# Time mixing of an RWKV-7 layer: six slots per pair of heads in place of eight

## The chip, the cores and the metric

The kernel runs on one core of a Trainium2 chip. The metric is the time of one execution on the device, in microseconds (us). Before the change it is 2622.2 us, the median of three runs (2618.82 to 2623.88).

The engines of the core appear in the profile under short names: PE is the matrix engine (TensorE), PEld its loading of weights, DVE the vector engine, ACT the scalar engine, POOL GpSimd, SP the engine whose queue issues most of the DMAs. Each engine works through its own instructions in order and waits for the others by semaphores. Matmuls write to PSUM, which has eight banks; everything else lives in SBUF.

## The reference, cut to what matters

The model has two layers over 256 tokens of width 2048. The first layer mixes over time as below, the second by attention; each is followed by an MLP, and every sub-layer is shifted, scaled and gated by vectors made from `c` (adaLN). Only the time mixing matters here:

```python
def rwkv7_time_mix(h, mu, w_r, w_k, w_v, w_o, w0, w1, w2, a0, a1, a2,
                   g1, g2, k_k, k_a, r_k, ln_w, ln_b):
    ...
    r = xr @ w_r
    k = xk @ w_k
    v = xv @ w_v
    ...
    decay = jnp.exp(-jnp.exp(heads(w_log)))
    def step(S, inp):
        r_t, w_t, k_t, v_t, kk_t, a_t = inp
        sa = jnp.einsum('bhvk,bhk->bhv', S, -kk_t)
        S = (S * w_t[:, :, None, :] + sa[..., None] * (kk_t * a_t)[:, :, None, :]
             + v_t[..., None] * k_t[:, :, None, :])
        y = jnp.einsum('bhvk,bhk->bhv', S, r_t)
        return S, y
    ...
    _, y = lax.scan(step, S0, xs)
    ...
    y = ((y - mean) * lax.rsqrt(var + GN_EPS) * ln_w + ln_b)
    y = y + jnp.sum(r_h * k_h * r_k, axis=-1, keepdims=True) * v_h
    y = y.reshape(B, T, D).astype(h.dtype) * g
    return y @ w_o
```

There are 32 heads of 64 channels. The recurrence over tokens is written in chunks of 64: inside a chunk it is a triangular system, solved with an inverse; from chunk to chunk a 64 x 64 state is carried.

## The kernel before

**A pair.** The kernel takes two heads together, 128 channels on 128 partitions; there are 16 pairs (`NPAIR`). The class `Pair` (L78) writes the time mixing of one pair as a Python generator: each `yield` ends a step. There are three parts, `EARLY`, `INVERT`, `LATE` = 8, 12, 16 steps (L80). `early` (L152) makes decay, normalised keys and the tiles `kr`, `bh`, `kh`, `vp`, `bk`; the head sums of the keys and of the bonus (`pss`, `pbn`) are matmuls with a block of ones (`head_sums`, L138) on an operand split in two parts (`parts`, L142). `invert` (L228) forms the product `bh` x `kr`, takes its triangle, and builds the inverse by doubling in five levels of 32 x 32 products (`tiles`, L131); a level is two steps. At level 2 it also makes the masked product `mk` of `kh` and `kr`. `late` (L300) is the chain over the four chunks: the first product `g`, the inverse applied to it (`sa`), the output `y` and the next state `zs`; then the group norm of `y` (squares, head sums `var`, scale), the gate product `pg`, and the result in `v`.

**The slots.** The loop at L1019 sets the order of the work by hand. A pair starts `SLOTS` = 8 slots after the one before, so up to 4.5 pairs are under way; there are 8 x 16 + 36 = 164 slots. In a slot, each live pair issues one step: inverts first, then late steps, then early ones, the two `sums` steps of late at the end (L1027). Behind these steps follow dense matmuls to cover their latency: `proj_steps` (L962) gives the projections k and r of the next pair, 16 units of 6 matmuls a pair, two units a slot. `tc.issue_after` keeps this order in TensorE's queue. In the last 36 slots, the tail, the dense work is `out_steps` (L979), a part of the output projection, 56 units spread by `pace` (L1015). Behind a slot's work, in four slots of eight, `w_make` splits a half weight tile in two parts (`halves`, ACT L424 and DVE L427) and loads a further one; in six of eight, `ada` takes one step of the adaLN vectors of later layers (DVE L505), each with a 512 KB load into one of three buffers `rada`. `ADA_A` = 111 of these loads belong to this stage.

**PSUM.** The stage uses all eight banks: `pj` (projections, one), `ms` (two, by `psm`), `gr` (one tile of two banks, by `two`, L111), `iv` (one, by `corner`, L224), and `lt` (two, one bank per pair in `late`). In `late`, `lt` holds the chain's products, `y`, `var` and `pg`, so a pair holds its bank for 16 slots. In the tail the output projection takes over `pj`, `iv` and `gr`.

Of the kernel before, what the change touches and what calls it, by code (L numbers as in the profile page):

```python
# [25 lines left out]
C = 64  # L26
# [51 lines left out]
class Pair:  # L78

    EARLY, INVERT, LATE = 8, 12, 16  # L80
# [61 lines left out]
    def parts(self, src, t=None, func=AF.Copy, scale=1.0):  # L142
        nc = self.b.nc
        hl = self.b.pw.tile([P, 2, T], F32R, tag="sq", bufs=1, name="sq")
        nc.scalar.activation(hl[:, 0, :], src, func, scale=scale)
        if t is None:
            t = self.s()
            nc.scalar.activation(t, src, func, scale=scale)
        nc.vector.tensor_tensor(out=hl[:, 1, :], in0=t, in1=hl[:, 0, :], op=ALU.subtract)
        return hl  # L150

    def early(self):  # L152
# [25 lines left out]
        self.pc = pw.tile([P, 4, 1], F32, tag="pc", bufs=4, name="pc")  # L178
# [9 lines left out]
        self.bh, self.kh = s("bh", 2), s("kh", 2)  # L188
# [21 lines left out]
        nc.scalar.copy(self.even_odd(self.vp), self.by_chunk(pt, 2, C))  # L210
        yield
# [7 lines left out]
        pbn = b.psm()[:, :T]  # L219
        self.head_sums(pbn, rkp)  # L220
        nc.vector.tensor_tensor(out=v, in0=pbn, in1=v, op=ALU.mult)
        yield

    def corner(self, l):  # L224
        t = self.b.psm() if l == 5 or self.j >= NPAIR - 1 else self.b.pp.tile([P, 512], F32, tag="iv", bufs=1, name="iv")
        return t.rearrange("p (c t) -> p c t", t=H)[:, 0:4, :]

    def invert(self):  # L228
# [14 lines left out]
        ar = self.ar = s("ar", 3)  # L243
# [27 lines left out]
        for l in range(1, 6):  # L271
            xs = half("xs", 2)
            pi = self.corner(l)
            if l < 5:
                self.tiles(pi, als[:, l - 1], tt_, [(i, i) for i in range(4)])
                b.mark(nc.scalar.copy(xs, pi))
            else:
                self.tiles(pi, co, tt_, down)
                for i, K in enumerate(QS):
                    if i % 2:  # L280
                        b.mark(nc.scalar.copy(xs[K], pi[K]))
                    nc.gpsimd.tensor_copy(uf[K, :, H * (i % 2):H * (i % 2) + H], u[K])
            yield
            pi = self.corner(l)
            if l < 5:
                self.tiles(pi, xs, u, [(i, i) for i in range(4)])
                nc.vector.tensor_tensor(out=u, in0=u, in1=pi, op=ALU.add)
                tt_ = turned()
            else:
                self.tiles(pi, xs, u, up)  # L290
                for K in QS[::2]:
                    nc.scalar.copy(uf[K, :, H:C], pi[K])
            if l == 2:
                pt = self.two()
                self.each(pt, 0, P, lambda c: ch(kh)[:, c, :], lambda c: kr[:, c, :])
                mk = self.mk = self.big("mk", 3)
                nc.vector.tensor_tensor(out=self.even_odd(mk), in0=self.by_chunk(pt, 2, P), in1=ui, op=ALU.mult)
            yield

    def late(self):  # L300
# [18 lines left out]
        zs = None  # L319
        for c in range(4):  # L320
# [3 lines left out]
            g, sa = (pw.tile([P, C], F32, tag=n_, bufs=3, name=n_) for n_ in ("g", "sa"))  # L324
            if c == 0:
                value(0, True)
            else:
                both(pgs[c % 2], kr[:, c, 0:C], zs, self.at(c), False, False)
            b.mark(nc.scalar.copy(g, pgs[c % 2]))
            yield  # L330
# [24 lines left out]
            yield  # L355

        sq = self.parts(py, None, AF.Square)
# [3 lines left out]
        yield  # L361
# [3 lines left out]
        nc.vector.scalar_tensor_tensor(out=rg, in0=py, scalar=b.vec("ln_w", j), in1=rg, op0=ALU.mult, op1=ALU.mult)  # L365
        yield
        pg = bank[:, 0, :]
# [7 lines left out]
class Body:  # L375
# [3 lines left out]
    SLOTS = 8  # L379
# [359 lines left out]
    def layer_a(self, st, sp):  # L739
# [205 lines left out]
        with ExitStack() as s1:  # L945
# [6 lines left out]
            e01 = [pw.tile([P, 4, C + 1], F32, name=f"e01_{i}") for i in range(2)]  # L952
            self.uf = [pw.tile([P, 4, C], F32, name=f"uf_{i}") for i in range(2)]
            for e, u in zip(e01, self.uf):
                nc.vector.memset(e[:, :, 0:1], 1.0)
                nc.gpsimd.memset(u, 0.0)
# [3 lines left out]
            pairs = [Pair(self, j, v[:, j, :], tw, ta, tg, e01[j % 2]) for j in range(NPAIR)]  # L960
# [18 lines left out]
            def out_steps():  # L979

                for n in range(8):
                    self.split(self.y_hl, n, v[:, n, :])
                sums, raws = self.o_ps, deque()
                todo = ([((n,), 0, HK) for n in (0, 1)] + [((n,), HK, HK + 4) for n in (0, 1)] +
                        [((n,), 0, HK) for n in range(2, 8)] + [((n,), HK, KT - 2) for n in range(2, 8)] +
                        [((0, 1), HK + 4, KT - 2)])
# [9 lines left out]
                for ns, lo, hi in todo:  # L996
# [7 lines left out]
                    for n in ns:  # L1004
                        for kt in range(lo, hi, 2):
# [4 lines left out]
                            if len(ns) > 1:  # L1010
                                self.o_last.append(self.halves(*raws.popleft()))
# [3 lines left out]
            pace = (1,) * 12 + (1.25,) * 8 + (1.75,) * 8 + (2.5,) * 8  # L1015
# [3 lines left out]
            for slot in range(S * NPAIR + Pair.STEPS):  # L1019
                live = []  # L1020
                for j, pr in enumerate(pairs):
                    at = slot - S * (j + 1)
                    if 0 <= at < Pair.STEPS:
# [3 lines left out]
                        live.append((0 if at in inverts else 1 + (at < Pair.EARLY) + 2 * sums, -at, pr))  # L1027
# [9 lines left out]
                if slot < S * NPAIR:  # L1037
                    if slot % S == 0:
                        dense = proj_steps(pairs[slot // S])
                    todo = 16 // S  # L1040
# [342 lines left out]
```

## Time and profile before

| | |
|---|---|
| median of three runs | 2622.2 us |
| the profiled execution | 2616.31 us, its span 2614.5 us |
| TensorE clock granted, mean | 0.994 |
| instructions in the span | 58893 |
| read from HBM | 656.71 MB, 252 GB/s over the span |

All times inside the kernel are of the profiled execution, counted from the start of its span. A busy time is the union of an engine's instructions. A matmul's end is modelled and overlaps the next one's start; the distance from start to start is what a matmul costs TensorE. In a row of grouped instructions stand line, engine, operation, out<-in with shapes, the count, then busy us and mean ns of one, then idle time ahead of them and what ended it. A row of waits reads: who waited <- for whom: us in total, times, longest. fp32r is a format of 32 bits that TensorE reads in one pass; an operand is split into two such parts to keep its precision. An fp32 matmul shows as two records.

### The profile page before, as it was taken

How to read it: one execution, taken by the hardware profiler on the slowest of the kernel's cores; microseconds unless marked ns; L12 is line 12 of the kernel's file. 1: busy time of each engine (PE TensorE's matmuls, PEld its weight loads, DVE VectorE, ACT ScalarE, POOL GpSimd, SP SyncE). 2: the span in 40 equal slices, each digit the busy share in tenths (PEclk: the TensorE clock that was granted, in tenths of full speed). 3: DMA queues.
4: the chain of work that ended last, by engine and by line, in shares of the span. 5: the costliest groups of instructions: out<-in, count | busy, mean ns of one | idle time of the engine just before them, and what ended most of it. 6: DMA issues, size and time to landing. Idle time of an engine off the chain costs nothing.

```text
span 2614.5 us, 58893 instructions
## 1 busy us (share of the span) xinstructions
PE 2551.0 (98%) x24018; PEld 2233.3 (85%) x24018; DVE 2075.4 (79%) x3021; ACT 1375.4 (53%) x2535; POOL 215.5 (8%) x336
## 2 busy tenths in 40 slices
PE   7998999998999999999999999999999999999998
PEld 4778888887998888888888988887898888888887
DVE  6788998897889888888889897899896555555555
ACT  3346666664565354364465554565564454553554
POOL 1001333332100000000001000000100000000001
PEclk9999999998999999999999999999999999999999
DMA  9876666666869889999888688887776555555553
GB/s 355 311 265 196 214 225 208 223 197 199 291 215 333 324 326 341 325 330 338 319 314 285 210 281 326 310 270 260 251 237 223 191 186 186 190 188 188 191 186 129
DMA packets 207119, 662.65 MB, mean 253 GB/s; under 512 B 21248, under 2 KB 53632, under 8 KB 206848
## 3 DMA queue, kind: packets, MB, share of 16 engines
q1 hardware_dynamic: 205072, 657.02, 73.3%
q8 instruction: 188, 3.08, 0.5%
q10 hardware_dynamic: 1776, 1.87, 0.2%
q14 instruction: 83, 0.68, 0.1%
HBM read 656.71 MB, written 2.10 MB: 252 GB/s over the span
## 4 chain that ended last, share of the span: by engine, by line
PE 85%; DVE 7%; issue 3%; ACT 2%; DMA 2%; POOL 1%; DVEq 0%; ACTq 0%; SPq 0%; POOLq 0%
PE pj L458 42%; PE pj L460 21%; PE pj L447 3%; PE pj L448 3%; PE pj L449 3%; DVE wL L427 2%; DVE acc L505 2%; PE lt L104 2%; PE iv L135 1%; ACT wH L424 1%; PE o L447 1%; PE lt L369 1%; DMA rada<-w_ada 1%; PE gr L104 1%; PE o L448 1%
## 5 line engine op out<-in xcount | busy, mean ns | idle before, releaser
L427 DVE TENSOR_TENSOR wL<-raw,wH 128x1024 fp32r<-128x1024 f32 x771 | 945.2, 1227 | 336.1 <-ACT wH L424 334.0
L424 ACT CAST wH<-raw 128x1024 fp32r<-128x1024 f32 x771 | 805.3, 1045 | 719.8 <-PE pj L458 583.3
L458 PE MATMUL pj<-aHL,wH 128*128 128x512 f32 x2816 | 892.7, 398 | 1.1 <-DVE x L1096 1.1
L458 PE MATMUL pj<-hHL,wH 128*128 128x512 f32 x2048 | 644.3, 396 | 0.0
L460 PEld LDWEIGHTS pj<-aHL,wL 128*128 128x128 f32 x2816 | 531.3, 189 | 124.1 <-DVE wL L427 0.8
L460 PE MATMUL pj<-aHL,wL 128*128 128x256 f32 x2816 | 563.4, 281 | 0.4 <-DVE wL L427 0.4
L505 DVE SCALAR_TENSOR_TENSOR acc<-rada,ct,acc 128x1024 f32<-128x1024 f32 x360 | 466.3, 1295 | 9.0 <-DMA rada<-w_ada 8.2
L460 PEld LDWEIGHTS pj<-hHL,wL 128*128 128x128 f32 x2048 | 384.2, 188 | 91.2 <-DVE wL L427 0.8
L458 PEld LDWEIGHTS pj<-aHL,wH 128*128 128x128 f32 x2816 | 431.7, 188 | 8.6 <-issue 8.3
L460 PE MATMUL pj<-hHL,wL 128*128 128x256 f32 x2048 | 402.1, 278 | 0.4 <-DVE wL L427 0.4
L458 PEld LDWEIGHTS pj<-hHL,wH 128*128 128x128 f32 x2048 | 312.0, 189 | 1.3 <-DVE hHL L1142 1.1
L447 PE MATMUL pj<-aHL,wH 128*128 128x256 f32 (+1 forms) x896 | 263.2, 294 | 5.6 <-ACT k L975 4.0
L448 PE MATMUL pj<-aHL,wH 128*128 128x256 f32 (+1 forms) x896 | 253.9, 283 | 1.1 <-issue 1.1
L449 PE MATMUL pj<-aHL,wL 128*128 128x256 f32 (+1 forms) x896 | 252.6, 282 | 0.0
L595 POOL TENSOR_TENSOR ss<-ss,sq 128x256 f32<-128x256 f32 x56 | 50.9, 910 | 1582.3 <-ACT sq L594 1582.0
L447 PEld LDWEIGHTS pj<-aHL,wH 128*128 128x128 f32 x896 | 169.5, 189 | 10.7 <-ACT k L975 4.7
L1167 DVE SCALAR_TENSOR_TENSOR x<-pj,mod,x 128x256 f32<-128x256 f32 x256 | 123.3, 482 | 64.2 <-PE pj L460 61.2
L448 PEld LDWEIGHTS pj<-aHL,wH 128*128 128x128 f32 x896 | 169.4, 189 | 1.9 <-issue 1.3
L449 PEld LDWEIGHTS pj<-aHL,wL 128*128 128x128 f32 x896 | 170.0, 190 | 0.2
L1139 ACT ACTIVATE t<-t 128x256 f32<-128x256 f32 x112 | 46.9, 419 | 119.8 <-DVE t L1111 119.8
L1142 DVE TENSOR_TENSOR hHL<-t,hHL 128x256 fp32r<-128x256 f32 x128 | 53.8, 420 | 1.7 <-ACT t L1141 1.0
L1140 ACT ACTIVATE hHL<-t 128x256 fp32r<-128x256 f32 x128 | 52.9, 413 | 4.1 <-DVE t L641 3.1
(265 smaller groups left out, 2734.5 us busy)
## 6 DMA issues: line engine op xcount, KB each, us to landing
rada<-w_ada SPq DMA_DIRECT2D x320, 512.0 KB, 5.2
raw<-w_up SPq DMA_DIRECT2D x256, 512.0 KB, 4.5
raw<-w_down SPq DMA_DIRECT2D x256, 512.0 KB, 4.5
rada<-w_ada_kv SPq DMA_DIRECT2D x64, 512.0 KB, 6.2
rawa<-w_ada SPq DMA_DIRECT2D x32, 512.0 KB, 6.9
rawa<-w_ada_t SPq DMA_DIRECT2D x32, 512.0 KB, 7.5
raw<-w_k SPq DMA_DIRECT2D x32, 512.0 KB, 4.0
raw<-w_r SPq DMA_DIRECT2D x32, 512.0 KB, 5.1
```

The lines of the kernel that those rows point to most:

```text
L104: return self.b.nc.tensor.matmul(o[O], lhsT[K], rhs[K], start=start, stop=stop, tile_position=(K.start, O.start), skip_group_check=True)
L424: nc.scalar.copy(Hf, raw)
L427: eng.tensor_tensor(out=Lf, in0=raw, in1=Hf, op=ALU.subtract)
L447: nc.tensor.matmul(ps, H[:, i, :], a(kt)[:, 0, :], start=(first and kt == 0), stop=False)
L448: nc.tensor.matmul(ps, H[:, i, :], a(kt)[:, 1, :], start=False, stop=False)
L449: ins = nc.tensor.matmul(ps, L[:, i, :], a(kt)[:, 0, :], start=False, stop=(last and kt == KT - 1))
L458: nc.tensor.matmul(ps, w[kt // HK][0][:, kt % HK, :], a(kt), start=(kt == 0), stop=False)
L460: ins = nc.tensor.matmul(ps[:, 0, :], w[kt // HK][1][:, kt % HK, :], a(kt)[:, 0, :], start=False, stop=(kt == KT - 1))
L505: nc.vector.scalar_tensor_tensor(out=self.acc, in0=raw, scalar=ck, in1=self.acc, op0=ALU.mult, op1=ALU.add)
L1140: nc.scalar.activation(h[:, 0, :], t, AF.Square)
L1142: nc.vector.tensor_tensor(out=h[:, 1, :], in0=t, in1=h[:, 0, :], op=ALU.subtract)
L1167: nc.vector.scalar_tensor_tensor(out=x, in0=ps[:, i, :], scalar=self.mods[(layer, 5)][:, n:n + 1], in1=x, op0=ALU.mult, op1=ALU.add)
```

## The change

- A pair starts every six slots (`SLOTS` = 6) and has 34 steps, so there are 6 x 16 + 34 = 130 slots, with up to 5.7 pairs under way. The dense units of a pair are spread 3, 3, 2, 3, 3, 2; weight splits come in slots 1, 2, 4, 5 of six, adaLN steps in every slot.
- `LATE` has 14 steps. The first product of the chain, `g` of chunk 0, is issued in the inverse at level 4, in the tile `gr`; one step at the end of the chain is no longer a step of its own; `y` is copied from PSUM to SBUF, and squares and scaling read the copy; `pg` goes into `ms`. So a pair holds its bank of `lt` for 12 slots.
- The bonus sums `pbn` move one step ahead; `mk` is made at level 3 instead of 2; levels 4 and 5 of the inverse use `ms` (for the last pair but one level 3 too, for the last pair all).
- Buffers: `sq` 2, `pc` 5, `ar` 4, `bh` 1, one `e01` for all pairs.
- The output projection's early units take output tiles 0 to 3 first instead of 0 and 1.

```diff
-    EARLY, INVERT, LATE = 8, 12, 16
+    EARLY, INVERT, LATE = 8, 12, 14
...
-        hl = self.b.pw.tile([P, 2, T], F32R, tag="sq", bufs=1, name="sq")
+        hl = self.b.pw.tile([P, 2, T], F32R, tag="sq", bufs=2, name="sq")
...
-        self.bh, self.kh = s("bh", 2), s("kh", 2)
+        self.bh, self.kh = s("bh", 1), s("kh", 2)
...
         nc.scalar.copy(self.even_odd(self.vp), self.by_chunk(pt, 2, C))
+        pbn = b.psm()[:, :T]
+        self.head_sums(pbn, rkp)
+        nc.vector.tensor_tensor(out=v, in0=pbn, in1=v, op=ALU.mult)
         yield
...
-        pbn = b.psm()[:, :T]
-        self.head_sums(pbn, rkp)
-        nc.vector.tensor_tensor(out=v, in0=pbn, in1=v, op=ALU.mult)
         yield
...
-        t = self.b.psm() if l == 5 or self.j >= NPAIR - 1 else self.b.pp.tile([P, 512], F32, tag="iv", bufs=1, name="iv")
+        t = self.b.psm() if l >= 4 - (self.j == NPAIR - 2) or self.j == NPAIR - 1 else self.b.pp.tile([P, 512], F32, tag="iv", bufs=1, name="iv")
...
+            if l == 4:
+                g = self.g = b.pw.tile([P, C], F32, tag="g", bufs=3, name="g")
+                pt = self.two()[:, 0, 0:C]
+                for _, O in self.at(0):
+                    self.mm(pt, mk[:, 0, 0:C], self.vp[:, 0, :], O, O, True, True)
+                b.mark(nc.scalar.copy(g, pt))
             yield
...
-            if l == 2:
+            if l == 3:
                 pt = self.two()
                 self.each(pt, 0, P, lambda c: ch(kh)[:, c, :], lambda c: kr[:, c, :])
...
-            g, sa = (pw.tile([P, C], F32, tag=n_, bufs=3, name=n_) for n_ in ("g", "sa"))
-            if c == 0:
-                value(0, True)
-            else:
+            if c:
+                g = pw.tile([P, C], F32, tag="g", bufs=3, name="g")
                 both(pgs[c % 2], kr[:, c, 0:C], zs, self.at(c), False, False)
-            b.mark(nc.scalar.copy(g, pgs[c % 2]))
-            yield
+                b.mark(nc.scalar.copy(g, pgs[c % 2]))
+                yield
+            sa = pw.tile([P, C], F32, tag="sa", bufs=3, name="sa")
...
-            yield
-
-        sq = self.parts(py, None, AF.Square)
+                yield
+
+        out = s("y", 1)
+        nc.scalar.copy(out, py)
+        sq = self.parts(out, None, AF.Square)
         yield
         var = bank[:, 0, :]
         self.head_sums(var, sq)
-        yield
         rg = s("sl", 1)
         nc.scalar.activation(rg, var, AF.Ln, scale=1.0 / C, bias=b.col(C_GN))
         nc.scalar.activation(rg, rg, AF.Exp, scale=-0.5)
-        nc.vector.scalar_tensor_tensor(out=rg, in0=py, scalar=b.vec("ln_w", j), in1=rg, op0=ALU.mult, op1=ALU.mult)
         yield
-        pg = bank[:, 0, :]
+        nc.vector.scalar_tensor_tensor(out=rg, in0=out, scalar=b.vec("ln_w", j), in1=rg, op0=ALU.mult, op1=ALU.mult)
+        yield
+        pg = b.psm()[:, :T]
...
-    SLOTS = 8
+    SLOTS = 6
...
-                todo = ([((n,), 0, HK) for n in (0, 1)] + [((n,), HK, HK + 4) for n in (0, 1)] +
-                        [((n,), 0, HK) for n in range(2, 8)] + [((n,), HK, KT - 2) for n in range(2, 8)] +
-                        [((0, 1), HK + 4, KT - 2)])
+                todo = ([((n,), 0, HK) for n in range(4)] + [((n,), HK, HK + 4) for n in range(4)] +
+                        [((n,), 0, HK) for n in range(4, 8)] + [((n,), HK, KT - 2) for n in range(4, 8)] +
+                        [(range(4), HK + 4, KT - 2)])
...
-            pace = (1,) * 12 + (1.25,) * 8 + (1.75,) * 8 + (2.5,) * 8
+            pace = (1,) * 12 + (1.5,) * 6 + (1.875,) * 8 + (2.5,) * 8
+            units = (3, 3, 2, 3, 3, 2)
...
-                        live.append((0 if at in inverts else 1 + (at < Pair.EARLY) + 2 * sums, -at, pr))
+                        live.append((0 if at in inverts else 1 + (at < Pair.EARLY) + 2 * sums,
+                                     -at if at != Pair.EARLY + 8 else 0, pr))
...
-                    todo = 16 // S
+                    todo = units[slot % S]
...
-                if slot == 2 * S - 4:
+                if slot == 2 * S - 3:
                     self.ada_fill()
                 with self.behind():
-                    if slot % S in (1, 3, 6, 7):
+                    if slot % S in (1, 2, 4, 5):
                         self.w_make()
-                    if slot >= 2 * S and slot % S in (0, 1, 2, 4, 6, 7):
+                    if slot >= 2 * S:
                         self.ada()
```

More of the change, by code (lines that the diff above doesn't have):

```diff
@@ L177, in early @@
         nc.scalar.activation(e2, cum, AF.Exp)
-        self.pc = pw.tile([P, 4, 1], F32, tag="pc", bufs=4, name="pc")
+        self.pc = pw.tile([P, 4, 1], F32, tag="pc", bufs=5, name="pc")
         nc.gpsimd.tensor_copy(self.pc, e01[:, :, C:C + 1])
@@ L242, in invert @@
         pg = self.by_chunk(pt, 2, P)
-        ar = self.ar = s("ar", 3)
+        ar = self.ar = s("ar", 4)
         nc.vector.tensor_tensor(out=self.even_odd(ch(ar)), in0=pg[..., C:P], in1=ui[..., C:P], op=ALU.mult)
@@ L318, in late @@
         value = lambda c, start: both(pgs[c % 2], mk[:, c, 0:C], vp[:, c, :], time(c), start, False)
-        zs = None
+        zs, g = None, self.g
         for c in range(4):
@@ L951, in layer_a @@
             nc.scalar.copy(self.bones, self.cst("bones"))
-            e01 = [pw.tile([P, 4, C + 1], F32, name=f"e01_{i}") for i in range(2)]
+            e01 = pw.tile([P, 4, C + 1], F32, name="e01")
             self.uf = [pw.tile([P, 4, C], F32, name=f"uf_{i}") for i in range(2)]
-            for e, u in zip(e01, self.uf):
-                nc.vector.memset(e[:, :, 0:1], 1.0)
+            nc.vector.memset(e01[:, :, 0:1], 1.0)
+            for u in self.uf:
                 nc.gpsimd.memset(u, 0.0)
@@ L959, in layer_a @@
             self.ada_left = self.ADA_A
-            pairs = [Pair(self, j, v[:, j, :], tw, ta, tg, e01[j % 2]) for j in range(NPAIR)]
+            pairs = [Pair(self, j, v[:, j, :], tw, ta, tg, e01) for j in range(NPAIR)]
             def proj_steps(pr):
@@ L1009, in out_steps @@
                             yield
-                            if len(ns) > 1:
+                            if len(ns) > 1 and n < 2:
                                 self.o_last.append(self.halves(*raws.popleft()))
```

## The prediction

> **What bounds the kernel now.** I read the page first, then busy time by stage, then the order of TensorE's instructions inside the stage that the change touches, and its waits last.
>
> ```profile
> span 2614.5 us, 58893 instructions
> PE 2551.0 (98%) x24018; PEld 2233.3 (85%) x24018; DVE 2075.4 (79%) x3021; ACT 1375.4 (53%) x2535; POOL 215.5 (8%) x336
> ```
>
> The page says TensorE, but a share over the whole span tells nothing of one stage. The instructions of the tile lt, the chain's bank, give the stage its place (minimum, median and maximum ns, first and last start):
>
> ```profile
> L104 PE MATMUL lt<-ar,sa x256: 218/218/363, 271.6 to 674.0; 64*64 64x64 f32 x128
> ```
>
> The last chain product starts at 674 us. The first projection of the stage stands at about 202 us; the MLPs and the attention behind it are not touched. The busy times of stretches of the stage, in the columns PE, PEld, DVE, ACT, POOL, clock, DMA share, GB/s:
>
> ```profile
> 202.00:216.00 14.00, 11.79 (x97) 11.58 (x98) 11.03 (x24) 10.07 (x24) 0.57 (x2) 1.00 0.58 187
> 216.00:325.00 109.00, 101.64 (x2178) 92.00 (x2180) 93.92 (x156) 68.15 (x178) 36.56 (x49) 1.00 0.63 202
> 325.00:575.00 250.00, 245.24 (x5844) 221.62 (x5831) 225.15 (x402) 166.19 (x479) 89.87 (x119) 0.99 0.68 217
> 442.87:493.00 50.13, 49.97 (x1166) 45.23 (x1164) 45.79 (x83) 33.17 (x96) 17.78 (x24) 1.00 0.68 221
> 588.00:674.00 86.00, 77.67 (x1544) 68.03 (x1544) 66.83 (x110) 39.20 (x116) 14.22 (x23) 0.92 0.69 215
> ```
>
> The first row is pair 0's projections alone, before any pair is under way. The fourth is two pairs of the steady state: 25.07 us a pair, PE idle for 0.16 us in both. VectorE is busy 22.9 us a pair, 2.2 us from its own limit. So the steady state has hardly a wait to remove. What is idle lies at the ends: 7.4 us while the pairs start (216 to 325) and 8.3 us in the tail (588 to 674), where the clock is 0.92 as well. The change can win there, or by making TensorE's own work shorter. Where that work has fat is seen in the order of its instructions (start, duration):
>
> ```profile
> 440.15 0.50 PE L140 MATMUL ms<-sq,bones 128*128 128x256 f32 x2
> 440.50 0.28 PE L447 MATMUL pj<-aHL,wH 128*128 128x256 f32 x1
> ...
> 441.81 0.28 PE L449 MATMUL pj<-aHL,wL 128*128 128x256 f32 x1
> 442.01 0.34 PE L135 MATMUL ms<-u,xs 32*32 32x32 f32 x10
> ...
> 442.65 0.33 PE L104 MATMUL lt<-vp,mk 64*64 64x64 f32 x4
> ...
> 443.15 1.13 PE L369 MATMUL lt<-tg,lg 128*128 128x256 f32 x4
> 443.93 0.47 PE L447 MATMUL pj<-aHL,wH 128*128 128x256 f32 x1
> ...
> 445.65 0.45 PE L135 MATMUL iv<-tt,al 32*32 32x32 f32 x32
> 446.03 0.33 PE L104 MATMUL lt<-ar,sa 64*64 64x64 f32 x4
> 446.20 0.28 PE L104 MATMUL lt<-mk,vp 64*64 64x64 f32 x4
> 446.31 0.28 PE L104 MATMUL lt<-vp,bk 64*64 64x64 f32 x4
> ...
> 446.55 0.28 PE L104 MATMUL lt<-vp,mk 64*64 64x64 f32 x4
> 446.76 0.39 PE L447 MATMUL pj<-aHL,wH 128*128 128x256 f32 x1
> ...
> 448.39 0.45 PE L135 MATMUL iv<-u,xs 32*32 32x32 f32 x32
> ```
>
> Durations overlap, so starts are to be read. A slot is a block of 12 dense matmuls, a run of 32-wide products, one of 64-wide ones, sometimes a full-width one, then the next block. Inside a block a matmul starts every 0.119 us (440.50 to 441.81 is eleven steps), so twelve take 1.43 us.
>
> **The change part by part.**
>
> *Fewer slots.* 8 x 16 + 36 = 164 slots become 6 x 16 + 34 = 130. The same matmuls are issued; every change of shape is paid 34 times less. Its price per slot: the three blocks above take 1.51 us (440.50 to 442.01), 1.72 (443.93 to 445.65) and 1.63 (446.76 to 448.39), so 0.19 over 1.43 on average. The first product of a 64-wide run takes 0.17 (446.03 to 446.20) and the last 0.21 (446.55 to 446.76) against 0.11 to 0.12 inside it: 0.14. One pass of 32-wide products takes 0.38 with its end (445.65 to 446.03), two in a row 0.64 (442.01 to 442.65, one of them half as long): up to 0.12 saved where two passes share a slot, and ten passes a pair now fall on six slots instead of eight; I take 0.10. Together 0.43 us a slot, times 34: 14.6 us less. The low end leaves the 32-wide term out (11); the high end adds the one small wait that returns in each pair, 0.3 us (PEld ms L140, below), over 15 pairs: 19.
>
> ```profile
> PEld ms L140 <- DVE sq L149: 0.9, 3, 0.3
> ACT da L250 <- DVE ar L244: 1.1, 3, 0.4
> ```
>
> *The start.* A slot now has 16/6 = 2.67 dense units on average in place of 2, so 1.9 us of cover instead of 1.43 for the vector work that TensorE waits for while one or two pairs are alive:
>
> ```profile
> PE iv L135 <- DVE tt L264: 2.9, 3, 1.4
> ```
>
> Three such waits of about 1 us lose 0.5 us each, and the slots with few pairs are fewer. I take 2.4 us of the 7.4 idle; bounds 0 and 7.4. The two adaLN loads that are issued ahead come one slot before the first adaLN step, as they come four slots before it now; a late one would hold VectorE once, not the pairs.
>
> *The tail.* The output projection's 56 units lie over 34 slots, and 114/34 = 3.4 pairs' steps remain at its start where 100/36 = 2.8 did. But adaLN steps now come in every slot instead of three of four:
>
> ```profile
> L505 DVE SCALAR_TENSOR_TENSOR acc<-rada,ct,acc 128x1024 f32<-128x1024 f32 x23 | 30.7, 1335 | 0.0
> L427 DVE TENSOR_TENSOR wL<-raw,wH 128x1024 fp32r<-128x1024 f32 x16 | 21.5, 1344 | 0.0
> ```
>
> Of VectorE's 22.9 us a pair, 6 x 1.335 + 4 x 1.344 = 13.4 are these two; 9.5 belong to the pair. The first twelve tail slots have about 0.82 of the full number of pairs. VectorE per slot: 1.34 + 0.82 x 9.5/6 + 0.33 (a quarter wL) + 0.4 (a split) = 3.4 us; TensorE: 0.71 dense + 0.43 + 0.82 x 10.2/6 = 2.5 us (10.2 is 25.07 less 11.4 dense less 8 x 0.43). Before, the same sums give 2.7 and 2.2. The shortfall grows from 0.5 to 0.9 us a slot: 4 us more idle over twelve slots. Bounds: 8.3 less (all tail idle gone) to 10 more (nothing made up later). The slowed clock, 0.08 of 86 us = 6.9, I leave as it is.
>
> *New reuse of banks.* The two-bank tile gr was used in four slots out of eight, now in five consecutive slots of six: values, transposes, first inverse product, mk, and the new first chain product. The ms pair, besides z, key sums, bonus sums and last level, also takes level 4 (two uses) and the gate: eight uses in six slots against five in eight. Both add waits on PE, with everything in TensorE's queue behind them. The nearest rows are the copies that empty gr:
>
> ```profile
> L250 ACT COPY da<-gr 32x128 f32<-32x128 f32 x40 | 10.3, 257 | 3.4 <-DVE ar L244 2.8
> L252 ACT ACTIVATE co<-gr 32x128 f32<-32x128 f32 x20 | 5.3, 263 | 0.0
> L244 DVE TENSOR_TENSOR ar<-gr,csts 128x256 f32<-128x256 f32 x10 | 4.2, 418 | 0.0
> ```
>
> ar, then four da and two co: 0.42 + 6 x 0.26 = 2.0 us. From the inverse product to mk's first write TensorE has, by the spacings above, 0.6 of chain products, 0.3 of key sums, 1.5 of dense (a two-unit slot) and one 0.38 pass: 2.8 us. It fits with 0.8 to spare; I take 0.15 us a pair, 2 us in all, bounds 0 and 28 (rival 3).
>
> A rule speaks against this part: the Trainium skill, "Perfetto Trace Analysis", section Optimizing Tensor Performance (Matmuls), asks that independent groups of matmuls rotate through different PSUM banks, so that one's evacuation lies beside the next one's matmuls. By it the 2.0 us would stand open in every pair, 30 us in all, and the sum would turn positive; the trace before shows no such reuse from slot to slot with so long an evacuation, so it can't decide. I go by the 2.8 us of other work in between.
>
> *Edits with one answer.* The first chain product moves into the inverse with its two products and its copy, so nothing is added on TensorE; a late step goes. The copy of y out of PSUM is new on ScalarE, about the row below per pair; ScalarE is busy 33.17 of 50.13, and the squares behind it have the rest of a slot. If that cover went, it would cost 0.4 us a pair. Of late's VectorE operations the one that scales y now reads SBUF in the same form. The bonus sums come a slot earlier with room for their operand (sq twice). The gate load on SP's queue now waits for the gate product only one slot back; the raw loads queued behind it wait for younger work anyway, and five slots remain until it is used. Weight splits keep four a pair, adaLN six, hence the same DMAs: nothing. The output projection takes tiles 0 to 3 first and so needs iv at its unit 8 and gr at unit 24; pair 14 leaves iv in tail slot 7, pair 15 leaves gr in tail slot 16, both in time: nothing, or one wait of a slot (2.5 us) if not.
>
> ```profile
> L975 ACT COPY r<-pj 128x256 f32<-128x256 f32 x10 | 4.0, 400 | 0.0
> ```
>
> *Sum.* -14.6 - 2.4 + 4 + 2 = -11 us. The profiled execution took 2616.3 us (span 2614.5 and 1.8 around it), 5.9 below the median of 2622.2. Taken from the median: 2611, with a range of its own of 2604 to 2618.
>
> **The rivals.**
>
> 1. *TensorE's steady state is not as full as its busy time says.* PEld, the weight loads, is busy 45.23 of 50.13 us. If six pairs under way could fill that too, 2.45 us a pair for 15 pairs, 37 us, go: 2585. For it speaks that matmul durations overlap and their union hides holes; against it that starts stand 0.119 us apart with no hole but at changes of shape. Chance 0.03. This is how the Trainium skill, "Trainium Kernel Development and Optimization", section Performance Expectations, would have it read: it calls matmul busy time a bad metric for the distance to the roofline and weight-load busy time a good one. By that rule a tenth of the steady state is free; the spacing in the rows doesn't agree.
>
> 2. *The ends give more.* The tail gets no worse or loses all its 8.3 us, and half the start's 7.4 goes: 14.6 + 3.7 + 0 to 8.3, so 2604 to 2596; the clock's 6.9 may return with it. For it: the longest of the waits above is 1.4 us, and slots grow by 0.5 and more. Against: VectorE's sum in the tail. Chance 0.15.
>
> 3. *Slower, through gr.* If VectorE is a weight split and an adaLN step behind when the first inverse product is done, ar starts 1.34 + 1.34 us late, and the chain of 2.0 becomes 4.7 against 2.8 of cover: 1.9 us a pair on TensorE, over 15 pairs 28 us, so -14.6 - 2.4 + 4 + 28 = +15: 2637. It decides from a delay of ar over 0.8 us. For it: VectorE at 22.9 of a hoped 24.2, and the last early step and both big operations meet in one two-unit slot (about 5 us of vector work against 3 of TensorE's). Against: the next slot has three units and little vector work, and ar waits in the slot after that. Chance 0.15.
>
> 4. *VectorE becomes the limit.* Its 2.2 us of idle a pair are waits for TensorE's results that six slots don't shorten; the period stays at 25 us, and only start and tail change: -2.4 + 4 = 2624, or 2619 with a third of the slots' gain. For it: 22.9 us of work in a period of 24.2 to 24.4. Against: those waits have room to vanish when VectorE lags. Chance 0.17.
>
> **How the numbers follow.** Forecast 0.50, rivals 0.03, 0.15, 0.15, 0.17. A measurement of this kernel can tell about 0.2% from no change, 5 us: faster is below 2617, slower above 2627. Faster: nine tenths of the forecast, rivals 1 and 2: 0.63. Same: the rest of the forecast and nearly all of rival 4: 0.20. Slower: 0.17. The range goes from 2594 (rival 2 inside, rival 1 out) to 2628 (rival 4 and the lower part of 3 inside); some 0.17 is left out.
>
> **What would show it.** In the profile after: a steady pair in 24.1 to 24.5 us with PE idle below 0.3 us in it, dense blocks of 18 and 12 starting 0.119 apart; 130 slots from 202 to about 663 us. Wrong: waits of PE on gr or ms (ACT da, DVE s, DVE v) of over 0.5 us in every pair (rival 3); VectorE over 97% busy and PE waiting for tt (rival 4); PE idle in the tail far from 12 us; the time after the stage changing by more than 2 us.

## The result and the profile after

The change makes the kernel slower: 2642.14 us (2639.66 to 2646.08, six runs) against 2621.41 us (2618.82 to 2624.66, six runs), a ratio of 1.0079, 95% interval 1.0066 to 1.0092. That is 20.7 us more, where 11 less were forecast. The profiled execution took 2643.22 us. First its page, for the span and the busy times:

```profile
span 2641.4 us, 58918 instructions
...
PE 2551.6 (97%) x24018; PEld 2238.6 (85%) x24018; DVE 2082.9 (79%) x3020; ACT 1382.2 (52%) x2551; POOL 220.3 (8%) x336
```

TensorE was busy for as long as before (2551.0 us); the span grew by 26.9, all of it idle by these rows. To find it I cut the stage in two: the *front*, from pair 0's first product for the decay to the first matmul of the output projection, and the *tail*, from there to the last product into lt. Busy times of front and tail before (columns as in the prediction):

```profile
216.00:590.10 374.10, 361.80 (x8371) 327.18 (x8370) 334.17 (x587) 245.08 (x690) 127.27 (x169) 1.00 0.66 210
590.10:682.40 92.30, 83.97 (x1550) 74.40 (x1549) 72.97 (x117) 41.90 (x119) 14.22 (x23) 0.93 0.71 225
```

The same after the change, then two pairs of its steady state and the stretch that answers to 325:575:

```profile
218.50:613.60 395.10, 355.68 (x8074) 325.58 (x8073) 335.33 (x571) 246.23 (x683) 131.84 (x169) 0.97 0.62 198
613.60:705.00 91.40, 84.19 (x1814) 75.26 (x1812) 74.83 (x128) 45.43 (x140) 14.66 (x23) 0.94 0.70 227
...
470.88:527.97 57.09, 51.21 (x1231) 46.93 (x1229) 48.52 (x87) 35.17 (x102) 17.85 (x24) 0.97 0.63 198
...
325.00:575.00 250.00, 224.95 (x5336) 206.04 (x5335) 213.07 (x371) 156.39 (x448) 82.74 (x107) 0.98 0.63 199
```

The front holds the loss: 395.1 us against 374.1. TensorE idles for 39.4 us in it (395.1 less 355.68), before for 12.3; its clock fell from 1.00 to 0.97. A steady pair takes 28.5 us (57.09 over 2) and has 2.9 us of idle, where it took 25.07 and had 0.08. VectorE is not full: busy 48.52 of 57.09. The tail is no worse (idle 7.2 against 8.3). The rest of the span, 1936.4 against 1932.1, isn't touched by the change; the kernel before, profiled again with one edit in this stage (e3), gave 1935.8, so I read nothing into it. Nor into the start of the front, 218.5 against 216.0: it is 216.1 in e1 and 219.3 in e3.

The equal busy times hide two things, since a matmul at half the clock counts as busy for longer. By the records of the clock in the traces, stretches at half clock cost 15.4 us in front and tail (half their length), before 8.5. Without them TensorE works 424.5 us there (439.87 busy) against 437.2 (445.77 busy). So front and tail together are 20.1 us longer: 26.0 more idle, 6.9 more for the clock, 12.7 less work.

What TensorE, VectorE and ScalarE waited for after the change, from 350 to 560 us:

```profile
PE gr L104 <- ACT da L250: 8.4, 6, 2.1
PE ms L135 <- DVE tt L264: 3.6, 4, 1.1
...
DVE wL L434 <- ACT wH L431: 15.2, 8, 2.3
...
ACT da L250 <- DVE ar L244: 12.6, 7, 2.5
```

Before, in the same stretch, no wait on gr is among TensorE's, none on wH among VectorE's, and ScalarE waited 2.5 us for ar in all. TensorE's largest rows over the whole front after the change are these:

```profile
PE gr L104 <- ACT da L250: 13.5, 10, 2.1
PE ms L135 <- DVE tt L264: 8.2, 8, 1.8
PE iv L135 <- DVE tt L264: 5.2, 11, 2.0
```

All its waits on gr are 14.8 us there (none before), those on ms and iv 19.6 (6.6 before). So the wait on gr is less than half of the idle. One pair shows how these hang together (timeline; start, duration, engine):

```profile
506.39 0.67 PE L104 MATMUL gr<-kr,bh 64*64 64x128 f32 x16
...
509.41 0.45 PE L135 MATMUL iv<-u,xs 32*32 32x32 f32 x32
511.78 0.67 PE L104 MATMUL gr<-kr,kh 64*64 64x128 f32 x16 [1.92 <-ACT da L250]
...
506.27 1.22 DVE L434 TENSOR_TENSOR wL<-raw,wH 128x1024 fp32r<-128x1024 f32 x1
507.41 0.48 DVE L372 SCALAR_TENSOR_TENSOR sl<-y,vecs,sl 128x256 f32<-128x256 f32 x1
507.80 1.76 DVE L512 SCALAR_TENSOR_TENSOR acc<-rada,ct,acc 128x1024 f32<-128x1024 f32 x1
509.49 0.47 DVE L377 SCALAR_TENSOR_TENSOR sl<-v,vecs,sl 128x256 f32<-128x256 f32 x1
509.88 0.41 DVE L244 TENSOR_TENSOR ar<-gr,csts 128x256 f32<-128x256 f32 x1
...
512.83 2.02 DVE L434 TENSOR_TENSOR wL<-raw,wH 128x1024 fp32r<-128x1024 f32 x1 [2.21 <-ACT wH L431]
...
510.33 0.26 ACT L250 COPY da<-gr 32x128 f32<-32x128 f32 x1 [2.44 <-DVE ar L244]
...
511.47 0.26 ACT L250 COPY da<-gr 32x128 f32<-32x128 f32 x1
511.75 1.04 ACT L431 CAST wH<-raw 128x1024 fp32r<-128x1024 f32 x1
```

The inverse product is done at 507.06 (506.39 + 0.67). ar, which takes its triangle, starts at 509.88, 2.8 us later: a weight split and an adaLN step stand ahead of it on VectorE. ScalarE stands still for 2.44 us, since its first copy out of gr comes after ar; gr is empty at 511.73, 4.7 us behind the product, and mk's product, ready since 509.86, goes in. Behind the copies on ScalarE stands wH's cast, which has nothing to do with gr: it starts at 511.75, and VectorE, now free, waits 2.21 us for it. Both da and ar only read gr. The Trainium skill, "PSUM — Partial Sum Buffer", section PSUM bank collisions raise a hardware error, says that the compiler's scheduler puts a dependency between two engines' accesses to one bank and partition quadrant even if both read. The rows agree: ar, then da; and in e9 below, where da is written first, it is ar that waits for da (10.9 us from 350 to 560).

### The profile page after: what moved, and what is told of

It reads as the page before. It is cut to its first block, busy times and chain, and to the rows that moved or that the text cites. A ratio compares the mean times of both kernels' runs of the same rounds, so it can differ in the third digit from the quotient of the medians.

```text
span 2641.4 us, 58918 instructions
## 1 busy us (share of the span) xinstructions
PE 2551.6 (97%) x24018; PEld 2238.6 (85%) x24018; DVE 2082.9 (79%) x3020; ACT 1382.2 (52%) x2551; POOL 220.3 (8%) x336
## 4 chain that ended last, share of the span: by engine, by line
PE 81%; DVE 10%; issue 4%; ACT 3%; DMA 2%; POOL 0%; DVEq 0%; ACTq 0%; POOLq 0%; SPq 0%
PE pj L465 42%; PE pj L467 21%; DVE acc L512 3%; PE pj L454 3%; DVE wL L434 2%; PE pj L455 2%; PE pj L456 2%; PE lt L104 1%; ACT wH L431 1%; PE o L454 1%; PE m L804 1%; DVE tt L264 0%; PE o L455 0%; PE o L456 0%; DMA lw<-lora 0%
## 5 line engine op out<-in xcount | busy, mean ns | idle before, releaser
L1148 ACT ACTIVATE t<-t 128x256 f32<-128x256 f32 x112 | 46.9, 418 | 119.6 <-DVE t L1120 119.6
L1150 ACT ACTIVATE t<-t 128x256 f32<-128x256 f32 x128 | 53.3, 417 | 3.3
```

The source lines that it names most:

```text
L1150: nc.scalar.activation(t, t, AF.Square)
```

## The experiments

Four theories went into them. G: TensorE waits to write gr again (rival 3). V: VectorE has too much in one slot, and a wait removed at gr returns elsewhere. E: the other edits cost time, not the six slots. H, added with e9 and read back into the earlier runs here: ScalarE's whole queue stands behind the late ar, and what waits for ScalarE is late too. Each ratio is to the kernel before on the same chip (medians 2617.7 to 2620.2 us), with its 95% interval; one thousandth is 2.6 us.

**e1_copies_first.** After's kernel, with the six copies ahead of ar, so that ScalarE no longer waits for VectorE there:

```diff
-        ar = self.ar = s("ar", 4)
-        nc.vector.tensor_tensor(out=self.even_odd(ch(ar)), in0=pg[..., C:P], in1=ui[..., C:P], op=ALU.mult)
         da, co, u = half("da", 1), half("co", 2), half("u", 2)
...
                 nc.scalar.mul(self.even_odd(co[K]), pg[K, :, :, H:C], -1.0)
+        ar = self.ar = s("ar", 4)
+        nc.vector.tensor_tensor(out=self.even_odd(ch(ar)), in0=pg[..., C:P], in1=ui[..., C:P], op=ALU.mult)
```

> The changed kernel, with the six copies out of gr (da, co) written ahead of the masked product ar. In the profile after, TensorE stands for 0.8 to 2.2 us a pair before mk's product, until ACT's copies behind a late ar have emptied gr; ar starts 1 to 3 us after the inverse product is done. Theory G (the reuse of gr from slot to slot is what costs): the copies no longer wait for VectorE, so about 1.3 us a pair go, 15 pairs: 2642 - 20 = 2622, and the wait of PE gr on ACT da is gone or below 0.5 us. Theory V (VectorE's work is bunched in some slots, the waits only move to the next thing that VectorE makes): less than 8 us gained, 2634 to 2642, and the waits for tt and u grow by what gr loses. Theory E (not the six slots, the other edits cost): no change, 2638 to 2646.

2619.41 us, 1.0002 (0.9991 to 1.0014): 20 of the 20.7 us come back by an edit that adds and removes no instruction. Its front, and its waits from 350 to 560 us:

```profile
216.10:585.90 369.80, 346.42 (x8075) 318.61 (x8073) 333.85 (x570) 242.23 (x677) 141.35 (x169) 1.00 0.66 210
```

```profile
PE gr L104 <- DVE ar L250: 4.9, 5, 1.3
PE gr L104 <- ACT bk L221: 1.4, 5, 0.4
PE gr L104 <- ACT xs L274: 1.1, 1, 1.1
...
DVE wL L432 <- ACT wH L429: 1.3, 3, 0.5
```

Idle falls from 39.4 to 23.4 us, and at clock 1.00 the same matmuls are 9.3 us shorter (346.42 against 355.68). VectorE's wait for wH goes from 15.2 to 1.3. But TensorE's waits on gr hardly do: 7.4 us are left of 8.7, since ar is no earlier (2.80 us behind its product against 2.27; means here and below are over pairs 4 to 13), and gr is empty at 3.21 us in place of 4.12. It is the other waits that go: all the rest of TensorE's rows in this stretch sum to 2.6 us, after the change to 10.1.

**e2_weights_earlier.** Other slots for the weight splits, so that none is left in slots 2 and 5. The one of slot 1 stays, and it still stands ahead of ar:

```diff
-                    if slot % S in (1, 2, 4, 5):
+                    if slot % S in (0, 1, 3, 4):
```

> The changed kernel, with the weight splits in slots 0, 1, 3, 4 of six instead of 1, 2, 4, 5, so that no big VectorE operation but adaLN's stands in slots 2 and 5, which have two dense units. Theory V: VectorE's load by slot is then 3.9, 3.3, 2.6, 5.2, 4.1, 3.9 us by the durations of the trace before, against TensorE's 5.3, 3.9, 3.4, 5.1, 3.5, 3.0: most of the stalls go, 2642 - 25 = 2617 or below, the waits for tt at the slot after 5 and for gr alike. Theory G: ar comes about 1.2 us earlier where a weight split stood ahead of it, 2642 - 12 = 2630, the waits for tt stay. Theory E: no change, 2638 to 2646.

2633.31 us, 1.0054 (1.0039 to 1.0069): 6.6 us less than after. ar starts 2.06 us behind its product in place of 2.27 (read from the timeline); a little of VectorE's queue is gone, not all. The time is near G's 2630; V's 2617 is missed.

**e3_before_mk_next.** The kernel before, with mk one slot behind the inverse product, so that gr is reused as in after:

```diff
         tt_ = turned()
+        pt = self.two()
+        self.each(pt, 0, P, lambda c: ch(kh)[:, c, :], lambda c: kr[:, c, :])
+        mk = self.mk = self.big("mk", 3)
+        nc.vector.tensor_tensor(out=self.even_odd(mk), in0=self.by_chunk(pt, 2, P), in1=ui, op=ALU.mult)
         yield
...
-            if l == 2:
...
```

> The kernel before at eight slots, with one thing of the change alone: mk's product is made in the slot after the inverse product (it is made five slots after it), so gr is used again from slot to slot. In the trace before gr is emptied 3.0 to 3.5 us after the inverse product, and TensorE has about 2.8 us of other work until the next slot's product. Theory G: TensorE waits 0.4 to 0.7 us a pair and more where VectorE is late, 6 to 12 us in all: 2627 to 2634. Theory V and theory E: nothing, 2617 to 2625.

2612.31 us, 0.9970 (0.9960 to 0.9981): not slower, so G as I had put it falls. The timeline has gr empty 3.10 us behind the inverse product on average and mk's product starting at 3.38; TensorE's other work ends at 3.19 in nine of the ten pairs, so the reuse just fits, and a tenth of a us is lost where it doesn't. After the change gr is empty at 4.12, mk's product starts at 4.41, and the other work ends at 2.81 in eight of ten. Reuse from slot to slot costs next to nothing by itself; a late ar does.

**e4_eight_slots.** All other edits of the change, at eight slots (mk at level 2, the first chain product at level 5):

```diff
-    SLOTS = 6
+    SLOTS = 8
...
-            units = (3, 3, 2, 3, 3, 2)
+            units = (2,) * 8
-                    if slot % S in (1, 2, 4, 5):
+                    if slot % S in (1, 3, 6, 7):
-                    if slot >= 2 * S:
+                    if slot >= 2 * S and slot % S in (0, 1, 2, 4, 6, 7):
```

> The changed kernel at eight slots a pair: all its other edits (14 late steps, first chain product in the inverse, here at level 5 as gr is free in that slot, y copied out of PSUM, bonus sums a step earlier, the output projection's order), two dense units a slot, weight splits and adaLN steps as before, mk at level 2 as before. Theories G and V (six slots bring the waits): 2616 to 2625, the steady pair in 25.1 us. Theory E: 2635 to 2645.

2608.99 us, 0.9962 (0.9947 to 0.9977): E falls. Without the six slots the other edits gain 10 us. Front and tail:

```profile
218.80:592.10 373.30, 365.76 (x8390) 329.31 (x8388) 338.35 (x592) 251.98 (x705) 130.04 (x169) 1.00 0.67 210
592.10:669.30 77.20, 73.41 (x1497) 64.68 (x1495) 66.55 (x109) 39.80 (x117) 19.39 (x23) 1.00 0.79 255
```

The tail is 15 us shorter than before's; idle is 3.8 us in place of 8.3, and the clock is full. In the front idle is 7.5 us in place of 12.3. Which edit does it wasn't separated.

**e5_mk_apart.** After's kernel with mk's product ahead of the wait (level 1; with buffers mk 4, kh 1, sa 2, zs 3):

```diff
-            if l == 3:
+            if l == 1:
```

> The changed kernel with mk's product made at level 1 of the inverse, three slots after the inverse product instead of one; mk has four buffers (kh one, sa two, zs three, to make room in SBUF). The order ar, then the copies, stays. What theory G says of the stall, sharpened: gr is emptied 4.1 us after the inverse product (mean of ten pairs, ar 2.3 us late), and there is 2.9 us of other work until the next product in it. With three slots between them the wait of PE gr on ACT da is gone: about 25 us gained as with the copies first, 2612 to 2622. Theory V: mk's evacuation now stands in the slot with the most vector work, ahead of the values' product in gr; the wait comes back there, 2628 to 2645.

2633.84 us, 1.0046 (1.0030 to 1.0062): the wait of mk's product on gr is gone, yet only 9 of the 20.7 us are back. Its waits, 350 to 560 us:

```profile
PE pj L454 <- ACT k L982: 5.8, 5, 1.4
...
PE gr L104 <- DVE mk L303: 1.7, 4, 0.5
...
DVE wL L434 <- ACT wH L431: 17.7, 9, 2.3
...
ACT da L250 <- DVE ar L244: 16.8, 8, 2.5
```

This tells G from H. ScalarE still stands behind ar, and with it the cast wH and the copy of k, whose bank pj TensorE now waits for: 15.2 us in the front, whose idle only falls from 39.4 to 33.8. The time lies in the range that V had given (2628 to 2645), but V's wait, for mk's evacuation, is 2.0 us of the front. e5 takes away the direct wait and gets 9 us; e1 takes ScalarE out from behind ar, leaves most of the waits on gr, and gets 20. So the larger part is the queue behind ar. The difference, 11 us, is an estimate of it: two savings need not add.

**e6_no_ada.** After's kernel with `ADA_A` = 0. The adaLN steps of this stage are made behind it, so only the stage is compared (2742.25 us in all, a single execution).

> The changed kernel without the adaLN steps of this stage: they are all made after it, in one go ahead of the output projection, so the whole time is longer by their loads and sums and only the stage (first product of a pair to the first matmul of the output projection: 395 us in the changed kernel, 374 before) is to be compared. This halves VectorE's big operations. Theory V and theory G with the late ar both say that the stalls vanish: ar under 1 us after the product, PE idle in the front below 12 us, the front 355 to 362 us. If the copies and the chain of waits are too long by themselves, whatever VectorE has to do: PE idle stays above 25 us and the front above 375.

A stretch of its steady state:

```profile
325.00:525.00 200.00, 200.00 (x4796) 186.12 (x4788) 137.77 (x288) 142.41 (x414) 72.77 (x101) 1.00 0.31 100
```

TensorE doesn't idle at all, and pairs follow each other by 24.1 to 24.3 us. ar starts 0.37 us behind its product, and gr is empty at 2.22. So the six-slot order by itself delivers the period that was forecast; the adaLN steps spoil it. They take VectorE's time ahead of ar; their loads (the DMA share is 0.31 here, 0.63 after the change) and their small sums on TensorE went with them and weren't separated. V is half right: the work is there, but where it returns depends on the order around ar.

**e7_copies_weights.** e1 and e2 together.

> Copies first and the weight splits in slots 0, 1, 3, 4, both. Theory V: the second half of the waits goes with the evener load, 2619 - 10 = 2609 or below. Theory G: the weights helped only by making ar earlier (9 us), which no longer matters when the copies come first: 2616 to 2622.

2614.68 us, 0.9974 (0.9960 to 0.9988). Front and tail:

```profile
216.00:581.10 365.10, 346.04 (x8075) 318.62 (x8073) 320.64 (x571) 243.35 (x680) 127.01 (x169) 1.00 0.66 213
581.10:671.80 90.70, 82.56 (x1814) 73.19 (x1812) 75.30 (x129) 46.03 (x142) 15.79 (x23) 0.98 0.73 232
```

The front is 9 us shorter than before's, though it still idles 19.1 us in place of 12.3. The time lies between what V (2609 or below) and G (2616 to 2622) had said.

**e8_seven_slots.** Seven slots a pair (`units` (3, 2, 2, 3, 2, 2, 2), mk at level 1, the first chain product a step later, weight splits in slots 0, 2, 3, 6, adaLN steps in all but slot 4); ar still ahead of the copies.

> The changed kernel at seven slots a pair: units 3, 2, 2, 3, 2, 2, 2; mk at level 1 and the first chain product in the second half of level 4, so that gr is never used in the slot after the inverse product; weight splits in slots 0, 2, 3, 6, adaLN in all but slot 4, which evens VectorE's load to 2.5 to 3.7 us a slot. If what costs at six slots is the place of the reuse and of the vector work, and not the number of pairs under way, then PE waits as little as at eight slots and 16 slots fewer at 0.43 us are gained on the eight-slot version: 2609 - 7 = 2602, a steady pair in 24.6 us. If VectorE is the limit once the period comes near its 22.9 us, the period stays at 25.3 and the time at 2608 to 2618.

2669.50 us, 1.0177 (1.0153 to 1.0201), a miss of my own making. Its wait and its stretch from 300 to 540 us:

```profile
PE pj L454 <- ACT k L982: 25.0, 8, 3.4
```

```profile
300.00:540.00 240.00, 213.87 (x4783) 193.22 (x4778) 188.44 (x326) 134.75 (x398) 61.84 (x95) 0.91 0.58 184
```

With these units k's eighth unit ends inside a block, and the next unit needs the same bank at once, with k's copy late on ScalarE: 3.1 us each time, and the clock at 0.91.

**e9_seven_even.** The same with `units` (3, 3, 2, 2, 2, 2, 2), so that k ends with a block, and e1's order.

> Seven slots again, mended where the run before it failed: its units 3, 2, 2, 3 let the projection k end inside a block, and r's first matmul stood behind ACT's copy of k for up to 3.4 us (PE pj on ACT k, 21.6 us in 210). Now 3, 3, 2, 2, 2, 2, 2, so k ends with a slot; copies ahead of ar as well. Theory H (what costs is the queue that stands behind a late ar: first ACT's copies out of gr, then its casts wH, then VectorE's splits, then TensorE; not the number of pairs under way): no such wait at seven slots, a steady pair in 24.6 us, 2600 to 2608. Theory V (VectorE's load near the period is the limit): period 25.3 or more, 2609 to 2620.

2619.01 us, 1.0004 (0.9994 to 1.0015): no change against before. H had this run at 2600 to 2608, V at 2609 to 2620, so here V's range holds and H isn't enough. Pairs follow each other by 26.1 us on average, where 24.6 was expected, and the front has 21.5 us of idle. What holds it there wasn't found.

**e10_eight_copies, e11_copies_weights_mk, e12_copies_weights_ada.** e4 with e1's order; e7 with e5's; e7 with the adaLN steps 2, 1, 1, 1, 1, 0 over the six slots.

> The eight-slot version of the changed kernel (2609.0) with the copies ahead of ar. There ar came 1.0 us after its product and no wait of PE on gr was seen. Theory H: nothing to gain, 2606 to 2612. Theory V: nothing either. If the order by itself costs or gains something beyond the waits, it shows here.

> Six slots with the copies first, the weight splits in slots 0, 1, 3, 4, and mk's product three slots after the inverse product. Left in the run without the last (2614.7) were waits of PE gr on DVE ar, 3.5 us in 210. Theory H: those 3.5 us go, 15 pairs 4 to 6 us less: 2608 to 2611. Theory V: mk's evacuation meets the slot with the most vector work: 2615 to 2622.

> Six slots with the copies first, the weight splits in slots 0, 1, 3, 4, and the adaLN step of slot 5 moved to slot 0, which then has two. By the durations of the trace before VectorE has then 5.2, 3.3, 2.6, 5.2, 4.1, 2.6 us in the six slots against TensorE's 5.3, 3.9, 3.4, 5.1, 3.5, 3.0. Theory V: the last waits in slots 5 and 0 go, a steady pair in 24.5 us, 2604 or below. Theory H: the bunching was no longer what waits, 2610 to 2618.

2611.15 us, 0.9969 (0.9958 to 0.9979); 2611.91 us, 0.9975 (0.9964 to 0.9985); 2615.65 us, 0.9989 (0.9978 to 1.0000). At eight slots the order of ar and copies brings nothing: ar starts 1.0 us behind its product there, and the next product into gr 7.0. At six slots neither moving mk nor the adaLN steps brings more than e7 has; e12 lies in H's range (2610 to 2618) and not in V's (2604 or below).

**e13_six_ada99, e14_eight_ada99.** e11 and e4 with twelve adaLN steps moved from the tail to behind the stage, to see whether VectorE holds the tail:

```diff
-    ADA_A = 111
+    ADA_A = 99
```

> The best six-slot version (copies first, weight splits in slots 0, 1, 3, 4, mk three slots after the inverse product: 2611.9) with 99 adaLN steps in the stage instead of 111, so that the last twelve of the tail's adaLN steps are made by the MLP. If VectorE holds the tail: 12 x 1.3 us of its work go, the tail shortens from 92 to 84 us or less, 2600 to 2606, unless the MLP gives it back. If TensorE's own work holds it: the tail stays within 2 us, 2609 to 2614.

> The eight-slot version of the changed kernel (2609.0) with 99 adaLN steps. PE is idle for 3.8 us in its tail of 77 us: at most 3 us are to be had, 2606 to 2611. If the MLP has no room for twelve more adaLN steps: 2612 or more.

2638.99 us, 1.0079 (1.0064 to 1.0094), and 2639.99 us, 1.0077 (1.0060 to 1.0094): e13 is 25 us above both of its ranges, e14 in the one for an MLP without room. In e13 VectorE has 14 us less in the tail (61.0 busy against 75.0 in e11) and the tail is as long (91.1 against 92.1): VectorE doesn't hold it. The loss is behind the stage, where the next one waits for weights:

```profile
690.00:760.00 70.00, 64.69 (x401) 58.10 (x400) 67.27 (x93) 36.83 (x60) 14.14 (x12) 0.95 0.86 295
760.00:900.00 140.00, 128.76 (x928) 113.44 (x928) 114.14 (x147) 63.68 (x95) 0.00 (x0) 0.96 0.77 270
```

## Why the prediction was wrong

**The failed step is "New reuse of banks".** It put 2.8 us of cover against a chain of 2.0 and took 0.15 us a pair, 2 us in all. The cover was right, 2.81. The chain was not: gr is empty 4.12 us behind the product on average (4.82 at most), since ar starts 2.27 us behind it, beyond the 0.8 from which rival 3 decides. mk's product waited 13.5 us for gr in the front, where 2 were taken.

The chain of 2.0 left out any delay of ar, and the trace before already had one. In this pair of it the inverse product ends at 483.51:

```profile
484.99 0.42 DVE L244 TENSOR_TENSOR ar<-gr,csts 128x256 f32<-128x256 f32 x1
...
486.59 0.26 ACT L250 COPY da<-gr 32x128 f32<-32x128 f32 x1
```

ar starts 1.48 us behind it and gr is empty 3.34 us behind it; the means are 1.30 and 3.16. It cost nothing there, as gr was next used some 16 us behind the product. Against 2.8 us of cover it leaves 0.36 us open, 5 us over 15 pairs (an estimate), before the change makes ar any later.

Rival 3 had the mechanism (a weight split and an adaLN step ahead of ar), the place and nearly the total: 2637 us against 2642. The reason that I set against it, "ar waits in the slot after that", doesn't hold: in the timeline above the split runs from the inverse product's start, the adaLN step after it, and ar behind both. The sum used VectorE's average per slot; what counts is what is queued ahead of one instruction.

Two costs were in neither the step nor the rival. The first is the queue behind ar: TensorE's waits on ms and iv grew from 6.6 to 19.6 us in the front, and e1, which leaves 10.5 of the 14.8 us on gr there, takes them to 7.8 and gets 20 us back. The second is the clock, which the prediction took up for the tail alone ("I leave as it is"): the stretches at half clock cost 10.1 us in the front, before and in e1 1.7. The direct wait, priced at 28 us in rival 3, was 13.5. So the total of rival 3 came nearly true by luck: half of its price, with two other costs in the place of the rest.

**Fewer slots: right.** e7 and the kernel before have the same matmuls. Without the half clock TensorE works 425.2 us over front and tail in e7 (428.60 busy less 3.4) and 424.5 after the change, 437.2 before. These 12 to 13 us less lie in the bounds of 11 to 19, below the 14.6 taken. The period of 24.2 in e6 is that of "24.1 to 24.5".

**The start: nothing.** The first four periods sum to 86.0 us against 88.4, no more than fewer slots give; 2.4 were taken. In e1 and e7 they sum to 81.1 and 83.3, so the late ar costs there too, and two stretches at half clock (3.4 us) lie in the 86.0.

**The tail: wrong in sign, small.** Idle fell by 1.1 us where 4 more were forecast. VectorE's sum per slot was the reason, and e13 shows that VectorE isn't what the tail waits for.

**Edits with one answer:** e4 shows that together they aren't nothing but 10 us of gain at eight slots. Its idle over front and tail is 11.3 us against 20.6, and no stretch there has half the clock, which cost 8.5 before.

**The rule on banks.** The Trainium skill's "Perfetto Trace Analysis", section Optimizing Tensor Performance (Matmuls), asks for groups that rotate through different banks and so spoke against this part; at six slots the trace agrees with its sign. e3 bounds it: the same reuse is free when the bank is empty (3.10 us) before the next group's turn (3.19).

So the six slots are worth having only with ar's order mended, and then are no better than the other edits alone: e7 and e11 take 2615 and 2612 us (0.9974 and 0.9975 of before), e4, eight slots with the other edits, 2608.99 (0.9962). It is the lowest measured, but e3, one edit to the kernel before, has 0.9970, and the intervals of all four overlap.

## What to carry to other kernels

When a buffer is to be reused sooner, list by the timeline what stands ahead of the emptying instruction on its engine, not that engine's average load. Then list what stands behind the waiting one on the next engine: unrelated work queued there is late too. Where two engines empty one bank, let the one with the short queue go first: here the order of seven instructions was worth 20 us of 2620.

## What the hardware showed that I had not expected

Waits of two microseconds can go with half the clock. The stretch around one wait on gr after the change, cut where the granted clock changes:

```profile
476.00:484.10 8.10, 5.70 (x143) 5.14 (x144) 6.33 (x9) 5.56 (x20) 1.88 (x4) 1.00 0.61 190
484.10:487.51 3.41, 3.41 (x45) 3.02 (x35) 2.89 (x4) 2.01 (x5) 2.88 (x3) 0.50 0.15 58
487.51:495.60 8.09, 8.09 (x202) 7.49 (x202) 8.05 (x16) 3.46 (x11) 1.72 (x3) 1.00 0.69 213
...
480.69:484.10 3.41, 1.36 (x54) 1.11 (x55) 1.72 (x4) 1.93 (x7) 0.43 (x2) 1.00 0.88 284
```

TensorE waits 2.05 us for gr, up to 483.57. From 484.10 it gets half the clock for 3.41 us, at a cost of 1.7. In the 3.41 us ahead it was busy for 1.36, four tenths. Six such stretches lie in the front after the change, one before. The Trainium skill, "TensorE: Matmul & The Clock Gate", section What's actually happening, tells of a window of this length that halves the clock after an idle one; here a window with 1.36 us of work was enough, and the longest wait on gr in the front was 2.1 us. Cut into windows of 3.41 us, in step with the changes of the clock, this stage's sixteen traces have 35 windows at full clock with TensorE busy under half: 30 were followed by half the clock. Of 211 between 0.5 and 0.8, 20 were; of 1839 above, one. No run sets the busy share by itself, so the cause is read from this pattern.

The kernel before may owe some of its time to this as well. The mean clock over its runs beside e3 and e4 is 0.9921, in theirs 0.9951 and 0.9958. As an estimate, 0.0030 and 0.0037 of 2615 us are 8 and 10 us, as much as these two gained. In e3's trace the clock is also all that differs over front and tail: half clock costs 3.4 us in place of 8.5, while idle (20.0 against 20.6) and work (437.2 in both) are the same. In e4's, idle falls too, so the clock isn't all there. Why their clock stays up is open.
